# Two-layer hybrid encoder: the high and low parts of the MLP input side by side in one matmul of 512 columns

## The chip, the core and the metric

The kernel runs on one NeuronCore of a Trainium2 chip. Its engines are TensorE (PE, matmuls; the profile lists its weight loads apart as PEld), VectorE (DVE), ScalarE (ACT), GpSimd (POOL) and SyncE (SP, which issues the DMAs). Matmuls write PSUM, which has eight banks of 512 f32 a partition; all else lies in SBUF. The metric is the device time of one execution in microseconds. The kernel before takes 767.74 us, the median of 3 runs between 767.7 and 768.35.

## The reference, cut to what matters

Two layers, 256 tokens, model width 1024, f32. Each layer has a token-mixing half (projections, grouped attention, dilated attention, gates, output projection) and an MLP half; each half normalises its input and applies a shift, a scale and a gate that come from a vector `c`:

```python
ada = c_act @ w_ada[l] + b_ada[l]
sh1, sc1, gt1, sh2, sc2, gt2 = [a[:, None, :] for a in jnp.split(ada, 6, axis=-1)]
h = rms(x, g_mix[l]) * (1.0 + sc1) + sh1
parts = jnp.split(h @ w_in[l], IN_SPLITS, axis=-1)
...
x = x + gt1 * (mixed @ w_out[l])
h2 = rms(x, g_mlp[l]) * (1.0 + sc2) + sh2
x = x + gt2 * (jnp.square(jax.nn.relu(h2 @ w_ff1[l])) @ w_ff2[l])
```

`w_ff1` is 1024 x 4096 and `w_ff2` 4096 x 1024. The change concerns `relu(h2 @ w_ff1)` first of all.

## The kernel before

**Products in three parts.** The big products run in fp32r with each operand split in a high part (a rounded copy) and a low part (what is left): `mm3` (line 680) adds high x high, low x high and high x low, three matmuls into one PSUM region. A weight tile of 128 x 1024 is loaded by SP into one of six `wr` buffers, ACT writes its high part, DVE its low part (`split_next`, line 659), into one of 14 buffers of 8 KB a partition (`b8`) that other large tiles share.

**The MLP** (`mlp`, line 1137). The 4096 hidden columns come in eight blocks of 512. Block 0 (`ff1_first`) has another form. For blocks 1 to 7, `ff1(j)` (line 1171) makes two halves `u` of 256 hidden columns, and each of these of two groups `i` of 128: the weights are stationary (128 x 128), and the transposed input `h2` streams past them, 256 tokens a matmul. `wide` (line 1013) runs `mm3` over the eight k of the model width, so a group is 24 matmuls of 256 columns. The two groups fill the halves of one PSUM bank. ACT then applies Relu from PSUM, squares in SBUF and writes the high part of the hidden values, DVE the low part. `ff2_one` (line 1184) adds blocks into four accumulator banks, with matmuls of 512 columns in which the hidden values are stationary and the weights stream. On PE, ff1 of block j is followed by ff2 of block j-1.

`wide` is also what the gates (`gates`) and the branch projections (`ya`, and the `yb` loop of `mixer`) use, with other streamed tiles: `hT` (the mixers' input; the profile has ff1's `h2` under the name hT too), `oa` and `ob`.

**Layout of the split inputs.** `h_tiles` (line 713) makes two tiles, one of all high parts and one of all low parts, each of 8 k x 256 tokens. `make_h` (line 716) fills them: DVE normalises x, PE transposes four blocks of 128 x 128 into one PSUM bank, ACT (two blocks) and DVE (two blocks) apply scale and shift out of that bank, DVE writes the high and the low part. It runs for each half of the tokens `t` and each four k `g`.

**The order of the work** comes from a planner. All operations are recorded in program order with estimated costs (`Plan.cost`, line 234). `links` (line 273) finds which operation must wait for which: two that touch the same bytes of a tile, or, both on PE, the same PSUM tile. `run` (line 366) plays the program through with these costs; each engine takes the ready operation that is due first, and the times found set new due times for the next of four passes. The operations are then emitted to the engines' queues in order of the planned start, and each engine works through its queue in that order. `CFG` holds what steers the program order: `seq0` and `seq1` are the order of the mixer's pieces in the two layers (c chunks of the projection, u and v gates, a and b attention, y branch projection, w one tile of the `c` product), `post0` the order in which the first chunks are finished, and `ada_f0` and `ada_f1` how many tiles of the `c` product stand behind each block of the MLP. Such a tile is one 512 KB load and one DVE product with a sum (`ada_tile`, line 595).

Of the kernel before, what the change touches and what calls it, by code (L numbers as in the profile page):

```python
# [30 lines left out]
THETA = 10000.0  # L31
NQKV = 3072
AHEAD = 1
CFG = dict(ahead0=1, pscale="a",
  post0=(5, 2, 0, 1), s2k=7, r2k=8, ahead=1, last="k",
  dve_ss=0, hk=2,
  ada_f0=[4, 6, 1, 6, 3, 5, 0, 0, 0], ada_f1=[3, 1, 1, 1, 2, 0, 0, 0, 0],
  seq0="c3 a v w c4 w w w u u u w a a w w w w w w v w a w w v v w w w b w w w w w b y w w v y y y".split(),
  seq1="w u c2 w c3 u w w w u w w w c4 w a c5 w u a a w w a w w v b w v w w b w v w y w w v w y y y w".split())
WR = 6  # L40
NB8 = 14
WARM = 3
PASSES = 4
HOLD = 400

# [83 lines left out]
class Plan:  # L129


    def __init__(self, tc, pools):
        nc = tc.nc
        self.tc = tc
        self.real = dict(PE=nc.tensor, DVE=nc.vector, ACT=nc.scalar, POOL=nc.gpsimd, SP=nc.sync)
        self.ops = []
        self.tiles = {}
        self.group = None
        self.hold = 0
        self.soon = False  # L140
# [5 lines left out]
        self.size = dict(s2k=512, r2k=512, wr=1024, w2=2048, b8=2048, hT=2048, gtb=D, pr=512, ps=512,  # L146
                         ss=2, shg=16, gcol=8, rstd=8, st=6, ka=512, ob0=512, ob1=512)

    def lanes(self):
        return [Lane(self, n) for n in ("ACT", "DVE", "POOL", "PE", "SP")]  # L150
# [82 lines left out]
    @staticmethod  # L233
    def cost(e, op, outs, ins, k):

        free = lambda z: int(np.prod([c for _, c in z.ap][1:]))
        n = max(free(z) for z in outs[:1] + ins)
        if e == "PE":
            n = free(outs[0])
            if op == "matmul" and F32R not in (ins[0].dtype, ins[1].dtype):  # L240
                if n > 256 and ins[0].ap[0][1] == P:
                    return 3.3 * n, 3.3 * n + 250.0
                if ins[0].ap[0][1] != HD and outs[0].ap[0][1] != HD:
                    return 225.0, 475.0
                return 1.03 * n, 1.03 * n + 250.0
            occ = 232 if n > 256 else 119 if n > 128 else 109
            return occ, occ + 205
        if e == "SP":
            return 480, max(free(z) * mybir.dt.size(z.dtype) * z.ap[0][1] for z in outs)
        if e == "POOL":  # L250
            occ = 400 + 150 * n if k.get("op") == ALU.pow else 440 + 1.7 * n
            return occ, occ + 60
        bank = "PSUM" in str(ins[0].space) if ins else False
        if e == "ACT":
            occ = (52 if bank else 93) + 0.834 * n
            occ += 40 * sum(pattern(k.get(z)) is not None for z in ("bias", "scale"))
            if k.get("accum_out") is not None:
                return occ + 93, occ + 308
            return occ, occ + 150
        if n <= 16:  # L260
            return 79, 204
        if op == "tensor_copy":
            occ = 68 + n * 0.521
        elif op == "tensor_scalar":
            occ = (187 if bank else 135) + n * (1.04 if bank else 0.521)
        else:
            occ = 69 + n / 0.96
        if op == "tensor_tensor_reduce":
            return occ + 6, occ + 191
        return occ, occ + 125  # L270


    def links(self):
        last = {}
        for o in self.ops:
            need = {}

            def wait(j, how, o=o, need=need):
                if j != o["i"]:
                    need[j] = max(need.get(j, 0), how)  # L280

            for kind, fs in (("r", o["r"]), ("w", o["w"])):
                for name, space, p0, p1, m in fs:
                    for j, jk, q0, q1, jm in last.get(name, ()):
                        if (kind == "r" and jk == "r") or p1 <= q0 or q1 <= p0:
                            continue
                        same = self.ops[j]["e"] == o["e"]
                        if space != "DRAM" and not jm & m:
                            if not ("PSUM" in space and o["e"] == "PE" and same):
                                continue  # L290
                        late = not same or o["e"] == "SP" or (o["e"] != "PE" and kind == "r")
                        wait(j, 2 if late else 1)
# [260 lines left out]
def encoder(ctx: ExitStack, tc: tile.TileContext, a: dict, out: bass.AP):  # L553
# [145 lines left out]
    def rms_x(l, w, t):  # L699
# [5 lines left out]
        for g in range(2):  # L705
# [4 lines left out]
                pe.transpose(ps[:, k * P : (k + 1) * P], xn[:, k * P : (k + 1) * P], ident)  # L710
            yield ps

    def h_tiles(l, w):
        return [tl("sbuf", [P, KT, S], F32R, "b8", NB8, f"hT{l}{w}{i}") for i in range(2)]

    def make_h(l, w, t, hT):
        v = shg[l, w]
        for g, ps in enumerate(rms_x(l, w, t)):
# [9 lines left out]
            hi, lo = (z[:, 4 * g : 4 * g + 4, t * P : (t + 1) * P] for z in hT)  # L728
            dve.tensor_copy(hi, hv)
            dve.tensor_tensor(lo, hv, f32(hi), op=ALU.subtract)  # L730

# [106 lines left out]
    def attention_tiles(l):  # L838
        T = {}

        z = [tl("sbuf", [P, 2, 4, S], F32, "b8", NB8, f"qk{l}{i}") for i in range(2)]
        T["qa"] = z[0][:, 0]
        T["b", 0], T["b", 1], T["b", 2] = z[0][:, 1], z[1][:, 0], z[1][:, 1]
        T["ka"] = tl("sbuf", [P, 1, S], F32, "ka", 1, f"ka{l}")
        v = tl("sbuf", [P, 2, 16, HD], F32, "b8", NB8, f"v{l}")
        T["va"] = [v[:, t, 12:14] for t in range(2)]
        T["vb"] = [v[:, t, 0:12] for t in range(2)]
        oa = tl("sbuf", [P, 2, 4, S], F32R, "b8", NB8, f"oa{l}")
        T["oa"] = (oa[:, 0], oa[:, 1])
        T["ob"] = [tl("sbuf", [P, 2, S], F32R, f"ob{i}", 1, f"ob{l}{i}") for i in range(2)]  # L850
        return T

    def chunk_post(l, c, t, ps, T):
# [14 lines left out]
    def qkv_chunk(l, c, hT, T):  # L868
        pss = [pb(f"qkv{l}_{c}_{t}") for t in range(2)]
        for j in range(4):  # L870
            wh, wl = weights_k(2)
            for t in range(2):
                for k in range(2):
                    kk = 2 * j + k
                    lh, ll = (z[:, kk, t * P : (t + 1) * P] for z in hT)
# [4 lines left out]

    def finish_o(ps, dst, cols):

        hi, lo = (z[:, cols, :] for z in dst)
# [15 lines left out]
    def att_a_pair(l, T, j, ops):  # L899
# [9 lines left out]
        for g in range(2):  # L909
# [8 lines left out]
                )  # L918
            dve.reciprocal(st[:, 2, :], st[:, 1, :])
            for t in range(2):  # L920
                scale_p(pr[:, t, :], st[:, 2, t : t + 1], CFG["pscale"])
            tp = pt(f"t{nm}")
            for kt in range(2):
                for t in range(2):
# [20 lines left out]
    def att_b_pair(l, T, hp, ops):  # L945
# [3 lines left out]
        for t in range(2):  # L949
# [10 lines left out]
            for hh in range(2):  # L960
# [9 lines left out]
                scale_p(pr, st[:, 2, t : t + 1], CFG["pscale"])  # L970
                prs[hh, t] = pr
        zs = []
        for hh in range(2):
# [39 lines left out]
    def wide(ps, i, wh, wl, xs, nk):  # L1013
        o = ps[:, i * S : (i + 1) * S]
        for k in range(nk):
            mm3(o, wh[:, k, :], wl[:, k, :], xs[0][:, k, :], xs[1][:, k, :], k == 0, k == nk - 1)

    fl = lambda z: z.rearrange("p a b -> p (a b)")  # L1020

# [115 lines left out]
    def mlp(l, h2):  # L1137
# [10 lines left out]
        def ff1_first():  # L1148
            hid = hid_tiles(0)
            ws = [weights_k(2) for _ in range(4)]  # L1150
            for t in range(2):
                ps = pa(f"f{l}_0_{t}")
                for kk in range(KT):
                    lh, ll = (z[:, kk, t * P : (t + 1) * P] for z in h2)
# [142 lines left out]
    for k in range(KT):  # L1297
        ada(2)
        v = shg[0, 0]
        h = s2k(f"h0_{k}")[:, :S]  # L1300
        for z in (h, hT[0][:, k, :]):
            act.activation(z, xT[:, k, :], AF.Identity, bias=v[:, 0, k : k + 1], scale=v[:, 1, k : k + 1])
        dve.tensor_tensor(hT[1][:, k, :], h, f32(hT[0][:, k, :]), op=ALU.subtract)
        for pair in ((0, 1), (2, 5)):
            w = weights(CFG["ahead0"])
            for i, c in enumerate(pair):
                wh, wl = (z[:, i * 512 : (i + 1) * 512] for z in w)
                for t in range(2):
                    lh, ll = (z[:, k, t * P : (t + 1) * P] for z in hT)
# [17 lines left out]
    for t in range(2):  # L1327
        pss = [pb(f"q1_{c}_{t}") for c in range(2)]
        for k in range(KT):
            if t == 0:  # L1330
                ws.append(weights())
            for c in range(2):
                lh, ll = (z[:, k, t * P : (t + 1) * P] for z in hT)
# [97 lines left out]
```

## Time and profile before

| | |
|---|---|
| median of 3 runs | 767.74 us |
| the profiled execution: span | 763.4 us |
| the profiled execution: its own time | 765.16 us |
| mean granted TensorE clock | 0.999 |
| MLP of layer 0 on PE | about 211 to 381 us |
| MLP of layer 1 on PE | about 584 to 760 us |
| matmuls, of these with hT (h2) streaming past weights | 4694, 2112 |

How to read the lines: in a group of instructions the tile written stands left of the arrow and the tiles read right of it, then the shapes, the count, the busy time in us and the mean in ns, and after the next bar the idle time of the engine just before. In the order of time the first two numbers are the start and the length in us of a merged piece, xN is the count of instructions in it, and the bracket says how long the engine sat idle before it and who released it. A matmul's own length includes the time in the pipeline, so a rate is read from starts and counts. In a view of stretches, each line has the stretch, its length, and for each of PE, PEld, DVE, ACT and POOL the busy time and the count, then the granted clock, the DMA share and GB/s. A line of waits says who waited for whom: us in total, times, longest.

All rows carry the line L549, that of the call that emits the plan, so tiles tell them apart.

### The profile page before, as it was taken

The page shows a single profiled execution, that of the slowest core. Times are in us where ns is not written, and L with a number is a line of the kernel's source. Part 1 is how long each engine was busy: PE and PEld are TensorE (multiplying, and loading weights), DVE is VectorE, ACT ScalarE, POOL GpSimd, SP SyncE. Part 2 cuts the span into 40 slices and gives each one's busy share as a digit, 9 for nine tenths or more (in the row PEclk, how much of TensorE's full clock was granted, in tenths as well). Part 3 has the DMA queues.
Part 4 walks back from the last instruction along what each step waited for, and adds up shares of the span by engine and source line. Part 5 has one row for each costly group of instructions (what it writes and reads, how often), then busy time and mean ns, then how long its engine had stood idle before and what let it go on. Part 6 is the DMA issues. An engine that isn't in the chain of part 4 may idle for free.

```text
span 763.4 us, 12235 instructions
## 1 busy us (share of the span) xinstructions
PE 746.6 (98%) x4694; PEld 650.9 (85%) x4694; DVE 571.8 (75%) x849; ACT 456.3 (60%) x728; POOL 68.8 (9%) x60
## 2 busy tenths in 40 slices
PE   8999999999999999999999999999999999999998
PEld 5788798998798889999878797889977999988997
DVE  5999898989799979545389997958778975455423
ACT  7568659894557565555256556699435864545520
POOL 0008650000000050000002111000000000000000
PEclk9999999999999999999999999999999999999999
DMA  8995488987469999654245666847733987565201
GB/s 325 368 377 198 145 269 306 335 296 253 169 246 393 377 365 360 248 192 175 83 138 194 248 228 244 329 153 234 249 138 126 368 331 251 193 220 193 84 1 55
DMA packets 50394, 180.52 MB, mean 236 GB/s; under 512 B 5624, under 2 KB 6048, under 8 KB 50336
## 3 DMA queue, kind: packets, MB, share of 16 engines
q1 hardware_dynamic: 50336, 179.75, 65.2%
q8 instruction: 36, 0.59, 0.3%
q14 instruction: 22, 0.18, 0.1%
HBM read 178.66 MB, written 1.06 MB: 235 GB/s over the span
## 4 chain that ended last, share of the span: by engine, by line
PE 76%; ACT 10%; DVE 8%; issue 3%; DMA 2%; SPq 0%; POOL 0%; ACTq 0%; DVEq 0%
PE ps L549 76%; DVE s2k L549 4%; ACT pr L549 4%; ACT s2k L549 3%; DVE w L549 2%; ACT w L549 2%; DMA wr<-in_w_x 2%; DMA x<-in_x 1%; DVE hT L549 1%; DVE rstd L549 1%; ACT G L549 0%; ACT hT L549 0%; ACT qk L549 0%; DVE pr L549 0%; ACT xT L549 0%
## 5 line engine op out<-in xcount | busy, mean ns | idle before, releaser
L549 DVE TENSOR_TENSOR w<-wr,w 128x1024 fp32r<-128x1024 f32 x236 | 285.5, 1227 | 85.5 <-ACT w L549 84.2
L549 ACT ACTIVATE w<-wr 128x1024 fp32r<-128x1024 f32 x236 | 245.6, 1058 | 115.3 <-PE ps L549 63.3
L549 PE MATMUL ps<-hT,w 128*128 128x256 f32 x2112 | 269.0, 285 | 0.0
L549 PEld LDWEIGHTS ps<-hT,w 128*128 128x128 f32 x2112 | 259.7, 191 | 5.5 <-issue 2.4
L549 PE MATMUL ps<-w,r2k 128*128 128x512 f32 (+1 forms) x792 | 178.5, 385 | 0.0
L549 PEld LDWEIGHTS ps<-w,r2k 128*128 128x128 f32 x792 | 144.3, 188 | 29.5
L549 PE MATMUL ps<-w,hT 128*128 128x512 f32 x672 | 163.3, 396 | 3.7 <-ACT hT L549 2.9
L549 PEld LDWEIGHTS ps<-w,hT 128*128 128x128 f32 x672 | 123.6, 188 | 32.6 <-ACT hT L549 4.6
L549 DVE CUSTOM_DVE_ANT_0 s2k<-wr,c_act 128x1024 bf16<-128x1024 f32 x96 | 116.9, 1235 | 1.7 <-DMA wr<-in_w_ada 1.0
L549 ACT ACTIVATE s2k<-ps 128x512 f32<-128x512 f32 (+2 forms) x108 | 57.5, 565 | 65.5 <-PE ps L549 54.6
L549 DVE TENSOR_TENSOR r2k<-s2k,r2k 128x512 fp32r<-128x512 f32 x28 | 19.6, 701 | 36.0 <-ACT r2k L549 36.0
L549 PE MATMUL ps<-w,mT 128*128 128x512 f32 x192 | 44.5, 391 | 0.0
L549 PEld LDWEIGHTS ps<-w,mT 128*128 128x128 f32 x192 | 35.8, 188 | 7.3
L549 POOL TENSOR_TENSOR rstd<-rstd,half 128x8 f32<-128x8 f32 (+1 forms) x20 | 33.3, 1679 | 66.9 <-DVE rstd L549 66.8
L549 ACT ACTIVATE pr<-pr,st 128x256 f32<-128x256 f32 (+1 forms) x64 | 36.0, 624 | 0.6 <-DVE st L549 0.5
L549 POOL TENSOR_TENSOR ss<-ss,half 128x1 f32<-128x1 f32 x8 | 4.4, 554 | 320.5 <-DVE ss L549 320.5
L549 ACT ACTIVATE s2k<-x 128x512 bf16<-128x512 f32 x16 | 10.0, 627 | 34.2 <-DVE x L549 30.8
L549 PE MATMUL ps<-consts,s2k 128*128 128x128 f32 x148 | 23.2, 279 | 6.2 <-ACT s2k L549 3.4
L549 DVE TENSOR_TENSOR s2k<-ps,gtb 128x512 f32<-128x512 f32 (+1 forms) x18 | 11.7, 658 | 23.1 <-PE ps L549 23.0
L549 PEld LDWEIGHTS ps<-consts,s2k 128*128 128x128 f32 x148 | 16.4, 140 | 13.5 <-ACT s2k L549 4.8
L549 POOL TENSOR_TENSOR s2k<-s2k,tabs 128x256 f32<-128x256 f32 (+1 forms) x20 | 21.2, 1081 | 56.8 <-ACT s2k L549 49.8
L549 PE MATMUL ps<-oa,w 128*128 128x256 f32 x192 | 24.7, 285 | 0.0
(81 smaller groups left out, 484.4 us busy)
## 6 DMA issues: line engine op xcount, KB each, us to landing
wr<-in_w_ff SPq DMA_DIRECT2D x120, 512.0 KB, 4.8
wr<-in_w_ada SPq DMA_DIRECT2D x96, 512.0 KB, 5.3
wr<-in_w_gate SPq DMA_DIRECT2D x32, 512.0 KB, 5.4
wr<-in_w_qkv SPq DMA_DIRECT2D x24, 512.0 KB, 3.7
wr<-in_w_x SPq DMA_DIRECT2D x16, 512.0 KB, 4.8
wr<-in_w_out SPq DMA_DIRECT2D x16, 512.0 KB, 5.2
wr<-in_w_y SPq DMA_DIRECT2D x8, 512.0 KB
wr<-in_w_ba SPq DMA_DIRECT2D x8, 512.0 KB, 4.5
```

Source lines behind the costliest of these rows:

```text
L549: getattr(self.real[o["e"]], o["op"])(*map(real, o["a"]), **{n: real(z) for n, z in o["k"].items()})
```

## The change

The high and the low part of a k now lie next to each other (`Split`): a tile has four k, and for each k 256 high and 256 low values. `ff1` uses this: for each k one matmul of 512 columns streams both parts past the high weights into a whole bank, and one of 256 columns streams the high part past the low weights into the bank's left half. The two halves of the bank are sums that still have to be added: ACT copies the right half to SBUF, DVE adds the left half to it, then Relu and square follow in SBUF. Each group `i` has a bank of its own. The gates, the branch projections and all products with three matmuls keep them, and read their parts from the new layout.

In the planner `links` lets a PSUM bank's writes and reads wait for each other across engines also where they touch different bytes; two reads still need not. The price of a per-partition bias or scale of an ACT instruction goes from 40 to 96 ns. `seq0`, `seq1`, `post0`, `ada_f0` and `ada_f1` have the same pieces in another order. `pscale` turns into a letter for each layer, with the same value.

```diff
-  post0=(5, 2, 0, 1), s2k=7, r2k=8, ahead=1, last="k",
+  post0=(5, 2, 1, 0), s2k=7, r2k=8, ahead=1, last="k",
-  ada_f0=[4, 6, 1, 6, 3, 5, 0, 0, 0], ada_f1=[3, 1, 1, 1, 2, 0, 0, 0, 0],
-  seq0="c3 a v w c4 w w w u u u w a a w w w w w w v w a w w v v w w w b w w w w w b y w w v y y y".split(),
-  seq1="w u c2 w c3 u w w w u w w w c4 w a c5 w u a a w w a w w v b w v w w b w v w y w w v w y y y w".split())
+  ada_f0=[5, 5, 0, 5, 3, 5, 0, 1, 1], ada_f1=[3, 0, 2, 0, 2, 0, 0, 1, 0],
+  seq0="c3 w a v w c4 w w u w u u w a w a w w w w w w v a w w v v w w w b w y w w w b w y w y v y".split(),
+  seq1="w u c2 w c3 u w c4 w u w w w a c5 w u a w w a w w v w b w v a b w w y w w v v w w w y y w w y".split())
...
-            occ += 40 * sum(pattern(k.get(z)) is not None for z in ("bias", "scale"))
+            occ += 96 * sum(pattern(k.get(z)) is not None for z in ("bias", "scale"))
...
                         if space != "DRAM" and not jm & m:
-                            if not ("PSUM" in space and o["e"] == "PE" and same):
+
+                            if "PSUM" not in space or (same and o["e"] != "PE"):
                                 continue
...
+    class Split:
+        def __init__(self, tiles, per):
+            self.tiles, self.per = tiles, per
+
+        def both(self, k):
+            return self.tiles[k // self.per][:, k % self.per]
+
+        def parts(self, k, cols):
+            z = self.both(k)
+            return z[:, 0, cols], z[:, 1, cols]
+
     def h_tiles(l, w):
-        return [tl("sbuf", [P, KT, S], F32R, "b8", NB8, f"hT{l}{w}{i}") for i in range(2)]
+        return Split([tl("sbuf", [P, 4, 2, S], F32R, "b8", NB8, f"hT{l}{w}{i}") for i in range(2)], 4)
...
+    def two_sums(ps, wh, wl, xs, nk):
+
+        for k in range(nk):
+            pe.matmul(ps, wh[:, k, :], xs.both(k).rearrange("p u n -> p (u n)"), start=k == 0, stop=False)
+            pe.matmul(ps[:, :S], wl[:, k, :], xs.both(k)[:, 0], start=False, stop=k == nk - 1)
...
         def ff1(j):
             hid = hid_tiles(j)
             for u in range(2):
-                ps = pa(f"f{l}_{j}_{u}")
+                r = s2k(f"r{l}_{j}_{u}")
                 for i in range(2):
                     wh, wl = weights_k(KT)
-                    wide(ps, i, wh, wl, h2, KT)
-                r = s2k(f"r{l}_{j}_{u}")
-                act.activation(r, ps, AF.Relu)
+                    ps = pa(f"f{l}_{j}_{u}{i}")
+                    two_sums(ps, wh, wl, h2, KT)
+                    ri = r[:, i * S : (i + 1) * S]
+                    act.activation(ri, ps[:, S:], AF.Copy)
+                    dve.tensor_tensor(ri, ps[:, :S], ri, op=ALU.add)
+                act.activation(r, r, AF.Relu)
                 act.activation(r, r, AF.Square)
                 split_hid(r, *hid[u])
             return hid
```

More of the change, by code (lines that the diff above doesn't have):

```diff
@@ L33 @@
 AHEAD = 1
-CFG = dict(ahead0=1, pscale="a",
-  post0=(5, 2, 0, 1), s2k=7, r2k=8, ahead=1, last="k",
+CFG = dict(ahead0=1,
+  post0=(5, 2, 1, 0), s2k=7, r2k=8, ahead=1, last="k",
   dve_ss=0, hk=2,
-  ada_f0=[4, 6, 1, 6, 3, 5, 0, 0, 0], ada_f1=[3, 1, 1, 1, 2, 0, 0, 0, 0],
-  seq0="c3 a v w c4 w w w u u u w a a w w w w w w v w a w w v v w w w b w w w w w b y w w v y y y".split(),
-  seq1="w u c2 w c3 u w w w u w w w c4 w a c5 w u a a w w a w w v b w v w w b w v w y w w v w y y y w".split())
+  ada_f0=[5, 5, 0, 5, 3, 5, 0, 1, 1], ada_f1=[3, 0, 2, 0, 2, 0, 0, 1, 0],
+  seq0="c3 w a v w c4 w w u w u u w a w a w w w w w w v a w w v v w w w b w y w w w b w y w y v y".split(),
+  seq1="w u c2 w c3 u w c4 w u w w w a c5 w u a w w a w w v w b w v a b w w y w w v v w w w y y w w y".split())
 WR = 6
@@ L42 @@
 WARM = 3
+PSCALE = "aa"
 PASSES = 4
@@ L146, in __init__ @@
         self.size = dict(s2k=512, r2k=512, wr=1024, w2=2048, b8=2048, hT=2048, gtb=D, pr=512, ps=512,
-                         ss=2, shg=16, gcol=8, rstd=8, st=6, ka=512, ob0=512, ob1=512)
+                         ss=2, shg=16, gcol=8, rstd=8, st=6, ka=512, ob=1024)
     def lanes(self):
@@ L727, in make_h @@
             hv = h.rearrange("p (k n) -> p k n", k=4)
-            hi, lo = (z[:, 4 * g : 4 * g + 4, t * P : (t + 1) * P] for z in hT)
+            hi, lo = (hT.tiles[g][:, :, i, t * P : (t + 1) * P] for i in range(2))
             dve.tensor_copy(hi, hv)
@@ L847, in attention_tiles @@
         T["vb"] = [v[:, t, 0:12] for t in range(2)]
-        oa = tl("sbuf", [P, 2, 4, S], F32R, "b8", NB8, f"oa{l}")
-        T["oa"] = (oa[:, 0], oa[:, 1])
-        T["ob"] = [tl("sbuf", [P, 2, S], F32R, f"ob{i}", 1, f"ob{l}{i}") for i in range(2)]
+        T["oa"] = Split([tl("sbuf", [P, 4, 2, S], F32R, "b8", NB8, f"oa{l}")], 4)
+        T["ob"] = Split([tl("sbuf", [P, 2, 2, S], F32R, "ob", 1, f"ob{l}")], 2)
         return T
@@ L874, in qkv_chunk @@
                     kk = 2 * j + k
-                    lh, ll = (z[:, kk, t * P : (t + 1) * P] for z in hT)
+                    lh, ll = hT.parts(kk, slice(t * P, (t + 1) * P))
                     mm3(pss[t], lh, ll, wh[:, k, :], wl[:, k, :], kk == 0, kk == KT - 1)
@@ L881, in finish_o @@
     def finish_o(ps, dst, cols):
-        hi, lo = (z[:, cols, :] for z in dst)
+        hi, lo = (dst.tiles[0][:, cols, i, :] for i in range(2))
         pv = ps.rearrange("p (h n) -> p h n", h=2)
@@ L920, in att_a_pair @@
             for t in range(2):
-                scale_p(pr[:, t, :], st[:, 2, t : t + 1], CFG["pscale"])
+                scale_p(pr[:, t, :], st[:, 2, t : t + 1], PSCALE[l])
             tp = pt(f"t{nm}")
@@ L969, in att_b_pair @@
                 dve.reciprocal(st[:, 2, t : t + 1], st[:, 1, t : t + 1])
-                scale_p(pr, st[:, 2, t : t + 1], CFG["pscale"])
+                scale_p(pr, st[:, 2, t : t + 1], PSCALE[l])
                 prs[hh, t] = pr
@@ L1015, in wide @@
         for k in range(nk):
-            mm3(o, wh[:, k, :], wl[:, k, :], xs[0][:, k, :], xs[1][:, k, :], k == 0, k == nk - 1)
+            mm3(o, wh[:, k, :], wl[:, k, :], *xs.parts(k, slice(0, S)), k == 0, k == nk - 1)
+    def two_sums(ps, wh, wl, xs, nk):
+        for k in range(nk):
+            pe.matmul(ps, wh[:, k, :], xs.both(k).rearrange("p u n -> p (u n)"), start=k == 0, stop=False)
+            pe.matmul(ps[:, :S], wl[:, k, :], xs.both(k)[:, 0], start=False, stop=k == nk - 1)
     fl = lambda z: z.rearrange("p a b -> p (a b)")
@@ L1153, in ff1_first @@
                 for kk in range(KT):
-                    lh, ll = (z[:, kk, t * P : (t + 1) * P] for z in h2)
+                    lh, ll = h2.parts(kk, slice(t * P, (t + 1) * P))
                     wh, wl = (z[:, kk % 2, :] for z in ws[kk // 2])
@@ L1300, in encoder @@
         h = s2k(f"h0_{k}")[:, :S]
-        for z in (h, hT[0][:, k, :]):
+        hi, lo = hT.parts(k, slice(0, S))
+        for z in (h, hi):
             act.activation(z, xT[:, k, :], AF.Identity, bias=v[:, 0, k : k + 1], scale=v[:, 1, k : k + 1])
-        dve.tensor_tensor(hT[1][:, k, :], h, f32(hT[0][:, k, :]), op=ALU.subtract)
+        dve.tensor_tensor(lo, h, f32(hi), op=ALU.subtract)
         for pair in ((0, 1), (2, 5)):
@@ L1308, in encoder @@
                 for t in range(2):
-                    lh, ll = (z[:, k, t * P : (t + 1) * P] for z in hT)
+                    lh, ll = hT.parts(k, slice(t * P, (t + 1) * P))
                     mm3(pss[c][t], lh, ll, wh, wl, k == 0, k == KT - 1)
@@ L1332, in encoder @@
             for c in range(2):
-                lh, ll = (z[:, k, t * P : (t + 1) * P] for z in hT)
+                lh, ll = hT.parts(k, slice(t * P, (t + 1) * P))
                 wh, wl = (z[:, c * 512 : (c + 1) * 512] for z in ws[k])
```

## The prediction

> **What bounds the kernel now.** I read the page's busy times first, then the chain that ended last, then the stretches of the layers, then the order of time on PE. The chain of waits has two pieces of PE alone that are 45% of the span:
>
> ```profile
> PE 746.6 (98%) x4694; PEld 650.9 (85%) x4694; DVE 571.8 (75%) x849; ACT 456.3 (60%) x728; POOL 68.8 (9%) x60
> ...
> 210.88 169.35 PE ps L549 x1064
> ...
> 584.28 175.38 PE ps L549 x1113
> ```
>
> They are the two MLPs: there only the rate of the matmuls counts. The attention halves (67 to 211 us, 395 to 584 us) are PE with small holes; the view of the stretches shows them, and the view of waits what PE waited for longest:
>
> ```profile
> 67.00:210.90 143.90, 141.45 (x996) 122.20 (x996) 129.93 (x217) 101.40 (x195) 32.38 (x26) 1.00 0.68 242
> 394.70:584.30 189.60, 185.17 (x1195) 159.37 (x1195) 155.33 (x266) 121.24 (x221) 16.69 (x12) 1.00 0.61 214
> ...
> PE ps L549 <- ACT s2k L549: 3.6, 7, 0.6
> ```
>
> PE is not busy for 143.90 - 141.45 = 2.45 and 189.60 - 185.17 = 4.43 us of them. The sum below starts from the profiled execution: span 763.4, its own time 765.16 us. The runs' median, 767.74, lies 2.58 above it; I take what is saved off the median.
>
> **The change, part by part.**
>
> *The matmuls of ff1.* The new form concerns 2 layers x 7 blocks x 2 x 2 column groups x 8 k = 448 steps; each had three matmuls of 256 columns and gets one of 512 and one of 256: 768 columns before and after, one matmul and one weight load fewer. The rates come from starts in the order of time on PE:
>
> ```profile
> 240.13 11.68 PE L549 MATMUL ps<-hT,w 128*128 128x256 f32 x96
> 251.65 11.17 PE L549 MATMUL ps<-w,r2k 128*128 128x512 f32 x48
> 262.65 11.66 PE L549 MATMUL ps<-hT,w 128*128 128x256 f32 x96
> ...
> 419.97 16.06 PE L549 MATMUL ps<-w,hT 128*128 128x512 f32 x70
> 435.87 0.60 PE L549 MATMUL ps<-consts,s2k 128*128 128x128 f32 x4
> ...
> L549 PE MATMUL ps<-w,r2k 128*128 128x256 f32 x48 | 5.6, 276 | 0.0
> ```
>
> An ff1 matmul takes (251.65 - 240.13)/96 = 0.1200 us, so a step 0.3600. A 512 of ff2 takes (262.65 - 251.65)/48 = 0.2292 us, one with hT stationary (435.87 - 419.97)/70 = 0.2271. The last group's 256s, which stream weights past hidden values, take (5.6 - 0.276)/47 = 0.1133. No row has 512 columns of hT streaming past stationary weights. Lower bound of the new step: 0.2271 + 0.1133 = 0.3404, saving 0.0196 x 448 = 8.8 us. Upper bound: each 256 columns keep the 120 ns of this pairing of operands, 0.3600, saving nothing. I take 0.2292 + 0.1200 = 0.3492, because ff2 alternates with ff1 on the same buffers and the remaining 256 is the very instruction of the first row: 0.0108 x 448 = **4.8 us**.
>
> The Trainium skill, page "TensorE: Matmul & The Clock Gate", section "Back-to-back issue gap", gives a warm matmul of N columns N/2.4 + 2.5 ns. That speaks against the change: one matmul fewer would free only 2.5 ns a step, an estimate of 1.1 us in all. The rows do not agree with it, 120.0 and 229.2 ns against its 109.2 and 215.8.
>
> *Turns in a PSUM bank.* The plan's dependences (`links`) gain: a read waits for earlier PE writes anywhere in its bank, a write for earlier reads. Before, the plan lets ACT read block 0 of four transposes (`make_h`) ahead of the fourth transpose. On the chip the bank turns out to be shared in turns anyway, and PE pays; in order of time, one such place with all engines, then PE at the others:
>
> ```profile
> 207.55 0.55 PE L549 MATMUL ps<-consts,s2k 128*128 128x128 f32 x3 [0.56 <-DVE s2k L549]
> 208.13 0.46 ACT L549 ACTIVATE s2k<-ps,shg 128x128 f32<-128x128 f32 x1 [2.25 <-PE ps L549]
> 208.65 0.77 PE L549 MATMUL ps<-consts,s2k 128*128 128x128 f32 x5 [0.55 <-ACT s2k L549]
> 209.01 0.41 DVE L549 TENSOR_SCALAR s2k<-ps,shg 128x128 f32<-128x128 f32 x1 [1.12 <-PE ps L549]
> 209.46 1.15 ACT L549 ACTIVATE s2k<-ps,shg 128x128 f32<-128x128 f32 x3 [0.87 <-DVE s2k L549]
> 210.88 0.50 PE L549 MATMUL ps<-w,hT 128*128 128x512 f32 x1 [0.31 <-DVE hT L549]
> ...
> 195.98 0.77 PE L549 MATMUL ps<-consts,s2k 128*128 128x128 f32 x5 [0.55 <-ACT s2k L549]
> ...
> 380.82 0.77 PE L549 MATMUL ps<-consts,s2k 128*128 128x128 f32 x5 [0.61 <-ACT s2k L549]
> 394.68 0.76 PE L549 MATMUL ps<-consts,s2k 128*128 128x128 f32 x5 [0.61 <-ACT s2k L549]
> ...
> 569.40 0.76 PE L549 MATMUL ps<-consts,s2k 128*128 128x128 f32 x5 [0.55 <-ACT s2k L549]
> 582.05 0.76 PE L549 MATMUL ps<-consts,s2k 128*128 128x128 f32 x5 [0.55 <-ACT s2k L549]
> ...
> 584.28 0.51 PE L549 MATMUL ps<-w,hT 128*128 128x512 f32 x1 [0.52 <-DVE hT L549]
> ```
>
> Three transposes, a read, then the fourth: 4 x 0.55 + 2 x 0.61 = 3.42 us of idle PE, the most this edit can give. With all four first, ACT starts one transpose (0.11 us) later, at 208.24, and ends at 208.70; DVE follows at 208.74 instead of 209.01, so hT is 0.27 us earlier. At two of the six places PE soon waits for hT (210.88 and 584.28), so there only 0.27 of 0.55 is won: 3.42 - 2 x 0.28 = **2.9 us**. At least: nothing, if the emitted order still interleaves.
>
> *The new evacuation.* Per column group of 256 one ACT copy and one DVE add, 56 of each; Relu now reads SBUF. By form:
>
> ```profile
> L549 ACT ACTIVATE r2k<-ps 128x256 fp32r<-128x256 f32 x8 | 2.8, 380 | 3.9 <-PE ps L549 3.9
> L549 DVE TENSOR_TENSOR r2k<-ps,r2k 128x256 fp32r<-128x256 f32 x8 | 3.2, 419 | 0.4 <-ACT r2k L549 0.4
> L549 ACT ACTIVATE s2k<-ps 128x512 f32<-128x512 f32 x96 | 54.8, 601 | 65.5 <-PE ps L549 54.6 <-DVE s2k L549 9.8 <-DVE rstd L549 0.9
> L549 ACT ACTIVATE s2k<-s2k 128x512 f32<-128x512 f32 x32 | 20.1, 628 | 0.7
> ...
> 211.00:263.00 52.00, 52.00 (x325) 46.87 (x326) 49.84 (x67) 32.24 (x42) 0.00 (x0) 1.00 0.90 342
> 263.00:380.80 117.80, 117.22 (x742) 106.21 (x740) 70.59 (x77) 60.67 (x76) 10.35 (x9) 1.00 0.66 245
> ```
>
> Half of it falls in layer 0: DVE 28 x 0.419 = 11.7 us, ACT 28 x 0.380 + 14 x 0.027 = 11.0 us. In that MLP DVE idles 169.8 - 120.4 = 49.4 us and ACT 76.9, so I cost it at **nothing**. The hidden values come 0.38 + 0.42 + 0.03 = 0.8 us later. ff2 of a block runs after ff1 of the next, 11 us on; only the last block has less, 24 matmuls of ff2 (5.5 us) in front of it against a chain of copy, add, Relu, square, copy, subtract of about 3.4 us. Without that cover it would cost up to 0.8 us a layer. The ff1 sums now take four banks a block instead of two; beside the four accumulators of ff2 four are left, and they rest through each ff2 stretch of 11 us.
>
> *Layouts at no cost.* hi and lo interleaved by k leave runs of 128 or 256 elements and the instruction counts as they were. What a stride can do to a matmul's rate, rows of oa and ob, with different strides, show:
>
> ```profile
> 164.49 8.80 PE L549 MATMUL ps<-oa,w 128*128 128x256 f32 x72
> 173.13 5.82 PE L549 MATMUL ps<-ob,w 128*128 128x256 f32 x48
> 178.79 16.07 PE L549 MATMUL ps<-w,mT 128*128 128x512 f32 x70
> ```
>
> 0.1200 against 0.1179 us; over the gates' 768 matmuls that is 1.6 us either way. I take zero.
>
> *The order.* The letters of both mixers and the ada places are permuted (25 and 8 ada tiles stay with the MLPs, each with one 512 KB load on SP's queue and one DVE reduction; by the third place of layer 0 ten instead of eleven), and the plan prices an ACT pointer operand at 96 ns, not 40. I take zero, and bounds of 6.9 us (2.45 + 4.43) either way: all PE idle of the mixers gone, or as much again.
>
> Sum: 765.16 - 4.8 - 2.9 = 757.5 for a profiled execution; from the median 767.74 - 7.7 = **760.0 us**.
>
> **The rivals.**
> - *The step is faster than I take it*, 0.3404 us: 767.74 - 8.8 - 2.9 = 756.0. For it: 512s with hT stationary do take 0.2271. Against: every 256 past stationary weights takes 0.118 or more.
> - *Columns alone set the rate*: 768 columns stay 0.3600 us, only the turns gain: 764.8. For it: 0.1133 x 2 is less than either 512, so length by itself saves nothing. Against: 0.1200 x 2 is 10.8 ns over 0.2292. By the page's rule above it would be an estimate of 763.7.
> - *The turns give nothing*, because the order is made anew and another read falls between transposes, or hT's chain of reads on ACT and DVE holds PE as before: 767.74 - 4.8 = 762.9. For it: the two places where PE already waits for hT.
> - *The mixers' new order costs as much idle again*: 760.0 + 6.9 = 766.9.
> - *Slower: DVE's in-order queue in the first MLP.* The add waits for ACT's copy, which waits for PE; behind it on DVE stand the low parts of weights, for which PE waits. Its rows:
>
> ```profile
> L549 DVE TENSOR_TENSOR w<-wr,w 128x1024 fp32r<-128x1024 f32 x23 | 28.1, 1223 | 1.9 <-ACT w L549 1.4
> ...
> DVE r2k L549 <- ACT r2k L549: 7.1, 5, 2.5
> ```
>
> From 211 to 263 us DVE is 49.84 of 52.00 busy; 8 adds of blocks 1 and 2 come in there. If each stood for the longest wait of the like subtract, 2.5 us, they take 8 x 2.92 = 23.4 us. Free are 2.2 us, one ada reduction fewer (1.2), and the splits made ahead: 23 against some 16 that PE uses (four for each of four stretches), 7 x 1.223 = 8.6. PE would be 11.4 us late, less 7.7: 771.4. It decides from 8 x (0.419 + w) = 19.7, a wait w of 2.0 us. Against it: the average wait of that row is 7.1/5 = 1.4, and the plan places the add after its data.
>
> **How the numbers follow.** Forecast 0.42 (by itself 757.5 to 762.5); faster step 0.13; columns alone 0.13; turns nothing 0.14; mixers' order 0.10, of which 0.07 within and 0.03 beyond; DVE queue 0.08. About 0.2% (1.5 us) is what a measurement of this kernel tells from no change. The first four are faster: 0.82; same 0.07; slower 0.08 + 0.03 = 0.11. The range reaches from the faster step with 1.5 us of the mixers' idle gone, 754.5, to just short of the mixers' case, 766.5.
>
> **What would show it.** The step: ff1 stretches of 64 matmuls that last 11.2 us instead of 11.52; 11.5 is columns alone, 10.9 the faster step. The turns: PE's waits for ACT s2k gone from 3.6 to under 1 us, transposes in fours. The evacuation: no idle PE within the MLPs; if DVE's queue fails, PE waits for "DVE w" between 211 and 263 us. The order: PE idle of the two mixers against 2.45 and 4.43 us. I am wrong if the ff1 stretches do not shrink, or if idle PE in mixers or MLPs takes up what they give.

## The result, and the profile after

| | before | changed |
|---|---|---|
| median | 767.89 us (4 runs, 767.7 to 768.35) | 755.82 us (4 runs, 755.61 to 756.11) |
| ratio to before | | 0.9842, 95% interval 0.9825 to 0.9859 |
| ratio, run again on another chip with more runs | | 0.9864, 0.9841 to 0.9887 (756.13 against 766.22) |
| the profiled execution: span, own time | 763.4, 765.16 | 754.0, 755.81 |

The change makes the kernel 12.1 us faster by the first comparison and 10.1 by the second; the forecast was 7.7. The profiled spans differ by only 9.4, because the profiled execution of before is one of its fast ones: over the chips used here before has taken 763.6 to 770.3 us. So traces explain some 9.4 us, and comparisons of times speak for the rest.

Where the trace gained is read from the starts of the same work in the order of time on PE. First before, then the changed kernel:

```profile
229.05 11.24 PE L549 MATMUL ps<-w,r2k 128*128 128x512 f32 x48
...
379.73 0.49 PE L549 MATMUL ps<-consts,s2k 128*128 128x128 f32 x3
...
552.90 15.39 PE L549 MATMUL ps<-w,mT 128*128 128x512 f32 x67
...
602.43 1.76 PE L549 MATMUL ps<-w,r2k 128*128 128x512 f32 x7
```

```profile
15.27 8.95 PE L551 MATMUL ps<-w,hT 128*128 128x512 f32 x31 [2.27 <-ACT hT L551]
...
177.23 15.16 PE L551 MATMUL ps<-w,mT 128*128 128x512 f32 x66
...
225.34 11.25 PE L551 MATMUL ps<-w,r2k 128*128 128x512 f32 x48
236.43 11.26 PE L551 MATMUL ps<-hT,w 128*128 128x512 f32 x64
247.52 11.15 PE L551 MATMUL ps<-w,r2k 128*128 128x512 f32 x48
258.51 11.45 PE L551 MATMUL ps<-hT,w 128*128 128x512 f32 x64
269.80 11.17 PE L551 MATMUL ps<-w,r2k 128*128 128x512 f32 x48
...
374.14 1.03 PE L551 MATMUL ps<-consts,s2k 128*128 128x128 f32 x8
...
543.87 1.32 PE L551 MATMUL ps<-w,mT 128*128 128x512 f32 x5
...
594.64 11.15 PE L551 MATMUL ps<-w,r2k 128*128 128x512 f32 x48
```

| stretch on PE | before | changed | difference |
|---|---|---|---|
| first projection to first mT, layer 0 (from 15.00 and 15.27) | 163.79 | 161.96 | -1.83 |
| to the first ff2, layer 0 | 50.26 | 48.11 | -2.15 |
| to the transposes of layer 1's input | 150.68 | 148.80 | -1.88 |
| to the first mT, layer 1 | 173.17 | 169.73 | -3.44 |
| to the first ff2, layer 1 | 49.53 | 50.77 | +1.24 |
| to the end | 160.97 | 159.36 | -1.61 |

A piece of 64 is one block of ff1, 32 matmuls of 512 columns and 32 of 256 in turns; its line names the shape of the first.

The MLPs (third and sixth row) gain 3.5 us: the ff1 blocks have 64 matmuls in 11.09 or 11.29 us instead of 96 in 11.50 or 11.52. But the mixers (first and fourth row) gain 5.3 us. Only 1.2 of that are pauses between transposes (the two of 0.61, in the fourth row), and the prediction had the mixers' order at zero. The fifth row loses.

The new evacuation is hidden as forecast. By form, and in the stretches of the first MLP:

```profile
L551 ACT ACTIVATE s2k<-ps 128x256 f32<-128x256 f32 x56 | 21.2, 378 | 42.3 <-PE ps L551 42.2
L551 DVE TENSOR_TENSOR s2k<-ps,s2k 128x256 f32<-128x256 f32 x56 | 23.6, 421 | 17.1 <-ACT s2k L551 17.1
...
207.00:259.00 52.00, 51.56 (x260) 43.58 (x261) 50.26 (x72) 34.91 (x51) 0.00 (x0) 1.00 0.91 343
259.00:375.00 116.00, 116.00 (x588) 98.15 (x586) 80.91 (x102) 65.85 (x95) 12.99 (x9) 1.00 0.71 251
```

378 and 421 ns against 380 and 419 taken; DVE is at 50.26 of 52.00, and PE is busy throughout the second stretch.

The transposes now come in eights, with nothing between. What PE waits for has moved from ACT's first read to hT:

```profile
192.91 1.03 PE L551 MATMUL ps<-consts,s2k 128*128 128x128 f32 x8
...
204.49 1.03 PE L551 MATMUL ps<-consts,s2k 128*128 128x128 f32 x8
205.28 1.17 PE L551 MATMUL ps<-w,hT 128*128 128x512 f32 x4
207.21 0.49 PE L551 MATMUL ps<-w,hT 128*128 128x512 f32 x1 [0.77 <-DVE hT L551]
207.94 0.73 PE L551 MATMUL ps<-w,hT 128*128 128x512 f32 x2 [0.23 <-DVE hT L551]
...
571.70 1.10 PE L551 MATMUL ps<-consts,s2k 128*128 128x128 f32 x8 [0.21 <-DVE s2k L551]
571.95 1.22 DVE L551 TENSOR_TENSOR w<-wr,w 128x1024 fp32r<-128x1024 f32 x1
572.39 0.46 ACT L551 ACTIVATE s2k<-ps,shg 128x128 f32<-128x128 f32 x1 [0.46 <-PE ps L551]
...
573.09 0.41 DVE L551 TENSOR_SCALAR s2k<-ps,shg 128x128 f32<-128x128 f32 x1
573.53 0.81 ACT L551 ACTIVATE s2k<-ps,shg 128x128 f32<-128x128 f32 x2 [0.68 <-DVE s2k L551]
...
574.95 0.50 PE L551 MATMUL ps<-w,hT 128*128 128x512 f32 x1 [1.45 <-DVE hT L551]
...
PE ps L551 <- DVE hT L551: 2.7, 4, 1.4
...
PE ps L551 <- ACT s2k L551: 0.2, 1, 0.2
```

Waits for "ACT s2k" fell from 3.6 to 0.2 us; those for "DVE hT" rose from 0.8 to 2.7. In layer 1 ACT and DVE take turns at reading the transposed blocks: ACT one (572.39), DVE one (573.09), then ACT again after a wait of 0.68 us for DVE. The matmul that needs hT starts 574.95 - 571.70 = 3.25 us after the first transpose. In layer 0 ACT reads its four blocks in a row, and there it is 207.21 - 204.49 = 2.72 us. From the transposes to the first ff2, layer 1 now takes 22.94 us instead of 21.48 (from 580.95 to 602.43 before): this is the loss in the fifth row. The weight split on DVE at 571.95 is not what makes the difference: with the old bank rule (below) a split stands there too, ACT reads in a row, and it is 2.78 us.

### The profile page after: what moved, and what is told of

It is laid out like the page before. It is cut to its first block, busy times and chain, and to the rows that moved or that the text cites. A ratio compares the mean times of both kernels' runs of the same rounds, so it can differ in the third digit from the quotient of the medians.

```text
span 754.0 us, 11447 instructions
## 1 busy us (share of the span) xinstructions
PE 739.9 (98%) x4246; PEld 629.9 (84%) x4246; DVE 595.4 (79%) x905; ACT 470.7 (62%) x784; POOL 70.2 (9%) x60
## 4 chain that ended last, share of the span: by engine, by line
PE 84%; DVE 7%; issue 4%; ACT 3%; DMA 1%; POOL 1%; SPq 0%; POOLq 0%; ACTq 0%; DVEq 0%
PE ps L551 84%; DVE s2k L551 4%; DVE w L551 2%; ACT s2k L551 2%; DVE rstd L551 1%; DMA x<-in_x 1%; ACT pr L551 1%; ACT w L551 0%; POOL s2k L551 0%; DVE x L551 0%; DVE hT L551 0%; ACT xT L551 0%; SPq L551 0%; POOL ss L551 0%; ACT c_act L551 0%
## 5 line engine op out<-in xcount | busy, mean ns | idle before, releaser
L551 PE MATMUL ps<-hT,w 128*128 128x256 f32 (+1 forms) x1664 | 263.8, 315 | 0.0
L551 PEld LDWEIGHTS ps<-hT,w 128*128 128x128 f32 x1664 | 234.4, 190 | 23.6 <-issue 2.6
L551 PEld LDWEIGHTS ps<-w,hT 128*128 128x128 f32 x672 | 126.2, 191 | 33.8 <-DVE hT L551 4.5
L551 ACT ACTIVATE s2k<-ps 128x512 f32<-128x512 f32 (+3 forms) x136 | 61.5, 479 | 64.0 <-PE ps L551 55.0
L551 ACT ACTIVATE s2k<-s2k 128x512 f32<-128x512 f32 (+1 forms) x62 | 38.3, 620 | 6.0 <-DVE s2k L551 5.2
L551 POOL TENSOR_TENSOR rstd<-rstd,half 128x8 f32<-128x8 f32 (+1 forms) x20 | 35.7, 1795 | 61.7 <-DVE rstd L551 61.7
L551 DVE TENSOR_TENSOR s2k<-ps,s2k 128x256 f32<-128x256 f32 x56 | 23.6, 421 | 17.1 <-ACT s2k L551 17.1
L551 DVE TENSOR_TENSOR s2k<-ps,gtb 128x512 f32<-128x512 f32 (+1 forms) x18 | 11.8, 659 | 20.5 <-PE ps L551 18.7
```

What stands on the lines that cost most here:

```text
L551: getattr(self.real[o["e"]], o["op"])(*map(real, o["a"]), **{n: real(z) for n, z in o["k"].items()})
```

## The experiments

Each ran beside the kernel before on the same chip; a ratio is to it. "Price" is that of an ACT pointer operand, "letters" are `seq0`, `seq1`, `post0` and the ada places. The theory: the form gives its PE time, the bank rule gives the waits between the transposes, and the order gives nothing. The rival: price and letters, by the order they make, give what is left.

**One part of the change put into the kernel before.**

*The bank rule.*

```diff
-                            if not ("PSUM" in space and o["e"] == "PE" and same):
+                            if "PSUM" not in space or (same and o["e"] != "PE"):
```

> Before with the new bank rule in the plan alone. Theory A (the prediction): 3.4 us of idle PE between the transposes go, some comes back as waits for hT: 767.9 - 2.9 = 765.0 us. Rival B (the time goes to the wait for hT, which DVE sets): 767 to 768 us, PE's wait for hT up by what its wait for ACT falls.

Measured: 762.42 us, ratio 0.9961 (0.9947 to 0.9975), 3.0 us below before's 765.45, as theory A has it. Its order of time on PE:

```profile
207.57 1.09 PE L549 MATMUL ps<-consts,s2k 128*128 128x128 f32 x8 [0.45 <-DVE s2k L549]
208.41 0.95 PE L549 MATMUL ps<-w,hT 128*128 128x512 f32 x3
210.41 0.50 PE L549 MATMUL ps<-w,hT 128*128 128x512 f32 x1 [1.05 <-DVE hT L549]
...
379.27 1.03 PE L549 MATMUL ps<-consts,s2k 128*128 128x128 f32 x8
```

The pauses are gone at all six places, at 379.27 with nothing in their place. At 210.41 the wait for hT is longer, 1.05 instead of 0.31 us, yet from these transposes to the first ff2 it takes 21.01 us instead of 21.50. By the stretches of the table above, the three that hold two places each (second, fourth and fifth row) are 0.90, 1.18 and 1.32 us shorter than before, and the other three are the same within 0.16.

*The form, with the new layout and evacuation.*

```diff
-                    wide(ps, i, wh, wl, h2, KT)
+                    ps = pa(f"f{l}_{j}_{u}{i}")
+                    two_sums(ps, wh, wl, h2, KT)
+                    ri = r[:, i * S : (i + 1) * S]
+                    act.activation(ri, ps[:, S:], AF.Copy)
+                    dve.tensor_tensor(ri, ps[:, :S], ri, op=ALU.add)
```

> Before with the new layout, the two matmuls a step and the new evacuation; bank rule, ACT price and letters as before. Theory A (the form gives what its matmuls show, 0.33 us in each of 14 blocks): 767.9 - 4.6 = 763.3 us, ff1 blocks of 11.1 to 11.3 us, no idle PE in the MLPs, and the transposes still in threes with six waits of PE of about 0.55 us. Rival B (the form only pays with the new plan, because the old ada places leave DVE no room for the adds): 766 us or more, with PE waiting for DVE between 211 and 263 us.

Measured: 764.71 us, ratio 0.9992 (0.998 to 1.0004): no change. Its order of time on PE, and the stretch from the first projection matmul to the first of mT:

```profile
243.84 11.26 PE L551 MATMUL ps<-hT,w 128*128 128x512 f32 x64
254.94 11.15 PE L551 MATMUL ps<-w,r2k 128*128 128x512 f32 x48
...
15.93:183.63 167.70, 162.08 (x1075) 138.65 (x1076) 152.82 (x253) 120.37 (x217) 38.08 (x30) 1.00 0.80 287
```

The block takes 254.94 - 243.84 = 11.10 us, so the rate is A's, and PE's two waits for DVE's weights stand at 73 and 86 us, not in the MLP where rival B has them. But the first mixer, in which nothing but the layout was changed, takes 167.70 us instead of 163.79. The layout is not the cause, since the products with oa and ob keep their rates, (177.98 - 169.82)/68 = 0.1200 and (183.63 - 177.98)/48 = 0.1177 us. What is left is the order: the plan is made anew for every edit, also far from it. Neither theory had this, and it means that a part alone doesn't measure itself.

*The price* (40 to 96) and *the letters*, each alone:

> Before with the price of an ACT pointer operand at 96 ns in the plan alone. Theory A (the prediction took zero for the order): 767.9 us within 1.5. Rival B (a truer price lets the plan place ACT's work so that PE waits less in the mixers): 765 us or less, idle PE of the mixers under 5 us.

> Before with the new letters of the mixers, post0 and ada places alone. Theory A (zero for the order): 767.9 us within 1.5. Rival B (the letters carry most of the 4.5 us that form and turns do not explain): 764 us or less. Rival C (they only fit the new price and form): 769 us or more.

Measured: 766.4 us, ratio 1.001 (1.0 to 1.002), and 767.04 us, ratio 1.0021 (1.0008 to 1.0033). Neither gains; the first mixer takes 165.20 and 165.79 us. A holds for the price, and the letters cost 1.6 us.

*Both together:*

> Before with the new price of ACT's pointer operands and the new letters together; form, layout and bank rule as before. Alone the price gave a ratio of 1.001 and the letters 1.0021. Theory A (the letters fit the plan that the new price makes): 762 us or less against 767 for before (ratio under 0.994), the first mixer, from the first projection matmul to the first of mT, about 161.5 us instead of 163.8. Rival B (the letters fit only the whole changed program, and any part put back makes another plan): ratio 0.998 to 1.003, first mixer 164 us or more.

Measured: 762.59 us against 766.52, ratio 0.9945 (0.9929 to 0.9962): 3.9 us faster, though each alone was none. The time is close to theory A's; the place is not, since its first mixer takes 163.41 us. With a span of 761.6 against 763.4 only half of the gain is in the traces: the first, second and fourth row are 0.38, 0.68 and 1.84 us shorter, but the first projection starts 1.12 us later (16.12 instead of 15.00). That start also differs between executions of one kernel, 15.27 and 16.10 in the changed one.

**The changed kernel with one part undone.**

> The changed kernel as it is, beside the kernel before on the same chip, whose runs have stood between 763.6 and 768.4 us. If the 9.4 us between the two profiled spans are the whole gain: 756 us against 765.5. If the 12.1 us between the first medians are: 753.4 against 765.5, or 755.8 against 767.9.

Measured: 756.13 us (754.95 to 758.75) against 766.22: 10.1 us, between the two expectations. This run is what the next ones are held against, by their ratios where the chip is another.

*The form, with the order kept.* At emission alone, the 512 becomes two 256s:

```diff
+                if o.get("two"):
+                    ps, wh, xx = map(real, o["a"])
+                    self.real["PE"].matmul(ps[:, :S], wh, xx[:, :S], start=o["k"]["start"], stop=False)
+                    self.real["PE"].matmul(ps[:, S:], wh, xx[:, S:], start=False, stop=False)
+                    continue
```

> The changed kernel with its planned order kept instruction by instruction; only where the 512-column matmul of ff1 is emitted, two of 256 columns are, into the same two halves of the bank. Theory A (a matmul has a fixed share of 10 ns here, whatever its columns): 448 x 10.3 ns = 4.6 us slower than the changed kernel, ff1 blocks of 11.5 us. Rival B (columns alone): no change. Rival C (DVE or ACT set the pace of ff1): no change in time, and waits of PE for them.

Measured: 759.43 us, ratio 0.9905 (0.9885 to 0.9924), 3.3 us slower than the changed kernel on the same chip. A stretch of one ff1 block:

```profile
236.67:248.19 11.52, 11.52 (x98) 11.52 (x96) 10.48 (x12) 9.29 (x13) 0.00 (x0) 1.00 1.00 369
```

11.52 us for 96 matmuls, as before the change, with the same columns, weights, evacuation and order: a step has a share that its columns don't set, and columns alone (rival B) is out. Whether it is the share of the matmul or of its weight load isn't shown, since no run leaves out one without the other. The loads are recorded as busy for the whole block here and before the change (11.52 of 11.52 us), and for 9.77 of 11.09 in the changed kernel's block at 236.43, so the load is a rival for these 10 ns that stays open.

Against the changed kernel run beside it the MLPs (third and sixth row) are 1.87 and 1.54 us longer. That 3.3 rather than 4.6 us show is partly layer 1's wait for hT: from the first mT to the first ff2 it takes 49.56 us here and 50.04 there. The runs, 758.28 to 761.31 against 754.95 to 758.75, don't tell 3.3 from 4.6 either.

*The old bank rule.*

> The changed kernel with the old bank rule in the plan. Theory A: the transposes fall in threes again, 2.9 us slower than the changed kernel. Rival B (the changed kernel already loses the gain again in waits for hT, 207.21 us and 574.95 us of its profile): within 1.5 us of it.

Measured: 757.88 us, ratio 0.9886 (0.9865 to 0.9906), 1.75 us slower: between A and B. The two ratios' intervals overlap, so the time alone doesn't show it; the stretches do. The three without a place are the same within 0.04 us, the second and fourth row are 0.82 and 1.33 us longer, and the fifth is 0.75 shorter. In the second row:

```profile
193.74 0.49 PE L551 MATMUL ps<-consts,s2k 128*128 128x128 f32 x3
194.78 0.77 PE L551 MATMUL ps<-consts,s2k 128*128 128x128 f32 x5 [0.55 <-ACT s2k L551]
...
209.01 0.50 PE L551 MATMUL ps<-w,hT 128*128 128x512 f32 x1 [0.18 <-DVE hT L551]
```

The pauses are back (0.55), at five places, and the wait for hT is smaller (0.18 instead of 0.77). At the sixth, before the MLP of layer 1, the transposes come in eights here too, and the matmul that needs hT starts 2.78 us after them (575.42 to 578.20) instead of 3.25.

*The old letters, and the old price.*

> The changed kernel with the old letters, post0 and ada places. Theory A (every re-plan moves the mixers by some us, and these letters are ones that fit): 2 to 4 us slower than the changed kernel, all of it before 205 us or between 385 and 560 us. Rival B (letters worth nothing): within 1.5 us.

> The changed kernel with the old price (40 ns) of an ACT pointer operand in the plan. Theory A (the new letters fit the new price: alone neither gained): 2 us or more slower than the changed kernel, in the mixers. Rival B (the letters alone do it together with form and bank rule): within 1.5 us.

Measured: 760.08 us, ratio 0.9914 (0.9895 to 0.9933), 4.0 us slower than the changed kernel; and 765.98 us, ratio 0.9975 (0.9959 to 0.9991). Against 0.9864 the latter is 1.1%, some 8.5 us: nearly the whole gain is gone. Stretches from the first projection to mT in the changed kernel (run again), with the old letters and with the old price, and what PE waited for in the last:

```profile
16.10:177.45 161.35, 159.63 (x1076) 138.94 (x1076) 151.44 (x253) 120.98 (x217) 38.09 (x30) 1.00 0.81 292
```

```profile
15.50:180.20 164.70, 161.96 (x1076) 140.42 (x1076) 152.17 (x254) 120.31 (x215) 33.92 (x30) 0.99 0.81 293
```

```profile
15.67:185.25 169.58, 162.72 (x1075) 139.88 (x1076) 154.11 (x254) 121.92 (x218) 35.43 (x30) 0.99 0.78 281
...
91.49 0.33 PE L551 MATMUL ps<-consts,s2k 128*128 128x128 f32 x1 [2.56 <-DVE s2k L551]
...
PE ps L551 <- DVE s2k L551: 5.5, 9, 2.6
```

161.35, 164.70 and 169.58 us for the same work of PE: 3.4 and 8.2 us more, most of what the old letters and the old price lose. Layer 1's mixer (fourth row) adds 2.0 and 1.8. With the old price PE stands 2.56 us for DVE at one place. Theory A, the fit of letters and price, holds.

**Two trials.** *Grouped:* in each group first the eight 512s, then the eight 256s, at emission alone.

```diff
+                if "low" in o:
+                    later.append((o["a"], o["k"]))
+                    if o["low"]:
+                        for a, k in later:
+                            self.real["PE"].matmul(*map(real, a), **k)
+                        later.clear()
+                    continue
```

> The changed kernel with its planned order kept, but in each group of ff1 the eight matmuls of 512 columns are emitted first and then the eight of 256. It asks for the rate of each alone with weights stationary and hT streaming. Theory A (13.3 ns over the columns for every matmul): 226.7 and 120.0 ns, 346.7 a step, 1.3 us faster than the changed kernel, whose steps take 346.7 and 352.7 in turns. Rival B (the prediction's lower bound, 227.1 and 113.3): 4 us faster. Rival C (a 512 of hT past weights takes 233 to 241 by itself, as some do in the changed kernel): slower by up to 3 us.

Measured: 756.24 us, ratio 0.9856 (0.983 to 0.9882), no different from the changed kernel. Its order of time on PE:

```profile
238.33 2.00 PE L559 MATMUL ps<-hT,w 128*128 128x512 f32 x8
240.16 1.11 PE L556 MATMUL ps<-hT,w 128*128 128x256 f32 x8
241.11 2.00 PE L559 MATMUL ps<-hT,w 128*128 128x512 f32 x8
...
249.50 11.15 PE L559 MATMUL ps<-w,r2k 128*128 128x512 f32 x48
```

(240.16 - 238.33)/8 = 0.2288 and (241.11 - 240.16)/8 = 0.1188; over the block (249.50 - 238.33)/32 = 0.3491 a step. None of the three theories: it is the 0.3492 of the prediction.

*The gates in the same form:*

```diff
-            wide(ps, i, wh, wl, hT, KT)
+            ps = bank(f"g{l}_{u}{i}")
+            two_sums(ps, wh, wl, hT, KT)
+            zi = z[:, i * S : (i + 1) * S]
+            act.activation(zi, ps[:, S:], AF.Copy)
+            dve.tensor_tensor(zi, ps[:, :S], zi, op=ALU.add)
```

> The changed kernel with the same form in the gates: 256 more steps, a bank a group, one more ACT copy and DVE add for each of 64 groups. Theory A (PE sets the mixers too): 256 x 10.3 ns = 2.6 us faster than the changed kernel. Rival B (in the mixers DVE has no room: 90% busy in layer 0 before, and 32 adds of 0.42 us are 13.4 us more): 3 us slower or more, PE waiting for DVE between 67 and 205 us. Re-planning alone has moved the mixers by up to 4 us either way.

Measured: 760.16 us, ratio 0.9905 (0.9882 to 0.9928): slower than the changed kernel by about 0.4%, and by 3.9 us than the grouped one on the same chip. The stretch from the first projection to mT, and its longest wait of PE for DVE's weights:

```profile
15.60:181.90 166.30, 162.88 (x948) 133.75 (x949) 154.88 (x265) 125.01 (x232) 39.09 (x30) 0.99 0.80 281
...
PE ps L551 <- DVE w L551: 1.5, 1, 1.5
```

128 matmuls fewer, and 166.30 us instead of 161.35. The gates have 32 groups, not the 64 of the expectation, and 16 of them fall in this stretch, so the adds are 16 x 0.415 = 6.6 us of DVE. DVE is busy for 154.88 us, 93% of the stretch, but in the changed kernel it was 94% (151.44 of 161.35). The time is B's; since re-planning alone has moved this stretch by as much, it isn't shown that the adds are the cause.

## Why the prediction was right, and where it was not

The direction and the range hold. 755.82 lies below the forecast's own range (757.5 to 762.5), and beside the first rival's 756.0, but not for its reason: the step is not 0.3404 us. By the second comparison the gain is 10.1 us, 2.4 more than the sum. What the sum lacks is the order, while the low end of the stated range was made mostly from a faster step, so that the time still falls within the range is in part luck.

- **The step of ff1: right.** Forecast 0.3492 us, measured 0.3466 (11.09/32) and 0.3528 (11.29/32), in grouped form 0.3491. The three rows that gave the bounds hold it, and 256s past stationary weights do not run at 0.1133 by themselves (0.1188 grouped). The gain in PE time, 448 x 0.0103 = 4.6 us, is the 4.8 forecast; in the time of the kernel the split form shows 3.3, which its runs don't tell from 4.6. Whether the matmul or its weight load carries the 10.3 ns is open.
- **The rule of the Trainium skill** ("TensorE: Matmul & The Clock Gate", "Back-to-back issue gap"), 2.5 ns a matmul over its columns, is given there for an isolated matmul, and does not hold for these fp32r streams: one matmul with its weight load fewer freed 10.3 ns a step, by the split form with everything else kept.
- **The turns: right for the rule alone, less in the changed kernel.** 2.9 forecast, 3.0 measured alone, and in the places as well: by the sum the second, fourth and fifth row gain 0.82, 1.22 and 0.82, and they gained 0.90, 1.18 and 1.32. In the changed kernel the rule is worth 0.82 and 1.33 in the first two, but loses 0.75 in the fifth row. There the step "hT is 0.27 us earlier" failed: counted from the first transpose, the matmul that needs hT starts after 3.25 us instead of 3.33, because ACT and DVE take turns, with one matmul fewer in front of it. PE's waits for hT grew at both places, from 0.31 to 1.00 us (0.77 and 0.23) and from 0.52 to 1.45. That "the chip" shares the bank in turns is more than the rows show: they show who released PE, in the program that ran.
- **The evacuation at nothing: right.** No wait of PE in the second stretch of the first MLP, 116.00 of 116.00; DVE's queue (the slower rival) shows no sign, for PE never waits for "DVE w" in the changed kernel's profile.
- **The layouts at no cost: right.** With the new layout oa and ob stream at 0.1200 and 0.1177 us, against 0.1200 and 0.1179.
- **"The order ... I take zero": this failed.** Price and letters together are worth 3.9 us alone; taking out the letters costs 4.0 us and the price some 8.5, which is more than the bound of 6.9 us. That bound was read from PE's idle time in the stretches, which hides most of what an order changes. From the first projection to the first mT it was, before:

```profile
15.00:178.79 163.79, 161.83 (x1075) 138.37 (x1076) 151.10 (x251) 120.54 (x216) 38.75 (x30) 1.00 0.81 292
```

The changed kernel, run again (161.35, 159.63, above), takes 2.44 us less, but PE's idle time fell only from 1.96 to 1.72 us: the rest was counted as busy, with the same matmuls. So the holes lie within the recorded lengths of matmuls. In part they are seen by form. Layer 0's attention, from its first score matmuls to mT (87.4 to 178.7 us before, 88.2 to 177.1 us changed), shows hardly any idle PE, yet first before, then the changed kernel:

```profile
L549 PE MATMUL ps<-consts,pr 128*128 128x128 f32 x64 | 11.8, 291 | 0.2
L549 PE MATMUL ps<-s2k,v 128*64 128x256 f32 x48 | 7.1, 393 | 0.2 <-ACT s2k L549 0.2
```

```profile
L551 PE MATMUL ps<-consts,pr 128*128 128x128 f32 x64 | 10.5, 278 | 0.7 <-ACT pr L551 0.7
L551 PE MATMUL ps<-s2k,v 128*64 128x256 f32 x48 | 6.5, 392 | 0.0
```

The same 64 transposes and 48 products hold PE 1.9 us less (11.8 + 7.1 - 10.5 - 6.5). Not every form gains: the 96 products with oa hold it 1.0 us more (12.9 and 13.9).

Multiplied, bank rule alone (0.9961), price with letters (0.9945) and the form in the changed order (0.9864/0.9905) give 0.9865, the changed kernel's 0.9864. That they close may be luck: undone one at a time, the parts come to 3.3 + 1.75 + 4.0 + 8.5 = 17.6 us, more than the whole, so they depend on each other. Which of the new letters matter was not tested. What also stays open is why executions of before spread over nearly 7 us, and which of it the 2.7 us between the profiled spans' difference and the first medians' are; before was profiled once.

## What to carry to other kernels

Count matmuls beside columns: with the same columns, order and data, each one dropped, together with its weight load, was worth 10 ns here, where PE alone set the pace. Where a planner makes the order, an edit is measured cleanly only with the order held (change the emitted form, not the plan), and a new cost in the planner is to be judged together with the program order that was chosen under it. Let the planner know what the program that it emits will wait for: reads placed between the transposes of one bank, at five or six places, cost 1.75 to 3.0 us.

## What was not expected of the hardware

The mixed stream of 512s and 256s has two rhythms. A whole block runs at 0.3466 us a step or at 0.3528, and the same block, ff1 of block 2 in layer 0, ran at 11.09 us in one execution of the changed program (236.43 to 247.52) and at 11.29 in another:

```profile
236.80 11.45 PE L551 MATMUL ps<-hT,w 128*128 128x512 f32 x64
248.09 11.17 PE L551 MATMUL ps<-w,r2k 128*128 128x512 f32 x48
```

So it isn't set by the addresses in SBUF or the order alone, which are the program's. In both executions the rhythms take turns from block to block, so the MLPs as a whole took the same time within 0.1 us. With the old letters, the old price or the form alone, however, each block of layer 1 took some 11.30 us (609.89 to 621.19 with the old letters). Grouped, every block took 11.17. Between the two rhythms lie 0.2 us a block, at most 2.8 us over the 14 blocks of an execution; what sets them stays open.
